# A hybrid decoder step on one core: sums, low parts and evacuations moved in four places

## The chip, the core and the metric

The kernel runs on one core of a Trainium2 chip. TensorE (PE) multiplies matrices into PSUM; VectorE (DVE), ScalarE (ACT) and GpSimd (POOL) work element by element, SyncE (SP) issues the DMAs. Each engine takes its instructions in the order of the program and waits for semaphores of the others. The metric is device time of one launch in microseconds, as the median over runs.

## The reference

The step takes 1024 prompt rows behind 16 meta rows and 8 sample rows, 1048 columns in all, at a width of 1024, in f32:

```
h += 0.5 * SwiGLU_1(rmsnorm(h))            # (silu(x @ wg) * (x @ wu)) @ wd, inner width 2816
u  = rmsnorm(h) @ w_in                     # q, f, i, g of HGRN2; z, x/B/C, dt of Mamba-2
HGRN2 (4 heads of 128): f = lb + (1-lb)*sigmoid(u_f), k = (1-lb)*sigmoid(-u_f), v = u_i, q = silu(u_q)
       S_t = diag(f_t) S_{t-1} + k_t v_t^T, o_t = S_t^T q_t, per-head RMSNorm, * silu(u_g)
Mamba-2 (8 heads of 64, 2 groups, state 128): conv(4) + SiLU, chunked scan
       h_t = exp(dt_t A) h_{t-1} + dt_t x_t B_t^T, y_t = h_t C_t + D x_t, grouped RMSNorm(y * silu(z))
h += concat(hgrn, ssm) @ w_out
h += 0.5 * SwiGLU_2(rmsnorm(h)); final RMSNorm
```

The samples use the same weights, and each has a state of its own: 4 x 128x128 for Mamba-2, read, updated by one step and written back. Outputs are the rows, and the states of prompt and samples.

## The kernel before

Columns are time, partitions are features. Every matrix product is done in three matmuls (`mm3`, L143 to L145): each operand is split into a high part (a cast by ACT) and a low part (what is left, by DVE), and high x high, high x low and low x high are added up in PSUM. Weights are split by `Left.hi` (ACT, L364) and `Left.lo` (DVE, L368), activations by `Blocks.cast` (ACT, L292) and `Blocks.low` (DVE, L298).

**FFNs.** An FFN works through its 2816 inner columns as 22 pairs (gate and up) of 128. A pair is done with seven products instead of eight (a Strassen-like scheme with the numbers 1, 5, 6, 7, 3, 4, 2): sums of weight blocks by `Left.sum_` (DVE, L360), sums of activations by `Blocks.sum_` (L287). Each product is two steps, one for each half c of the columns; a step is twelve matmuls. `Steps` is an order written out by hand: `S.before(i, fn)` issues fn before step i, and the instructions of an engine then run in that order. `Left.plan` sets when loads, sums and splits of a later pair are issued, relative to its first step s0. After a product `post` reads PSUM: product 1 is copied out by ACT (z, L450), 6 and 5 are added by DVE (v, L452; x, L457), 7 gives u1 (L459), 3 gives g1 (L462), each times the norm's factor r where it is complete (`times_r`, L445), 2 gives g0. In the first pair of an FFN, the products come half by half (1, 5, 2, 6, 7, 3 of the first half, then of the second, then 4 twice), since the second half's operands are still being made; there `post_first` holds back the reads of 5 and 2 until 6 and 3 are done. `first2` is the hand-written order of FFN2's first pair, in which `nf2.end` finishes the norm (L211 matmuls, then ACT's logarithm and exponential and DVE's L161 to L163). In `Hidden.jobs` the finished columns are stored (L538) by SP between the weight loads (L354).

**State-space stage.** Behind the input projection of x, B, C and dt a scan runs over nine chunks of 128 columns (`ssm_scan`). Outside the hand-written order a planner places the instructions of an engine by their dependencies. For a chunk SP loads the cumulated decays (L1085, L1092), ACT scales (L1111) and exponentiates them (L1112, L1121), DVE forms the weighted matrix (L1114), PE multiplies (L1118, L1124, L1132), and DVE adds up (L1125, L1126, L1129). PE's projections of HGRN head 0 (q, f, v) are placed between the chunks: `hgrn_project` evacuates each of three column chunks with ACT's Silu (q, L1256) or two Sigmoids (f and k, L1260, L1261). Silu, Sigmoid and Exp need different tables in ACT, and a change of table is an instruction of its own. After each projection three jobs of `K.jobs` are issued: job b updates the state of sample b (loads L1189 and L1190 by SP, L1191, L1195 and L1196 on POOL), reduces it against C (four L1198 on DVE, each writing a product and a sum) and stores it (L1199). The last job adds D x.

**Output.** `ssm_norm` normalises two groups (ACT squares, POOL adds them in L1233, PE sums over partitions in L1237, ACT and DVE finish), the second just ahead of `out_proj`, whose first four units use operands that do not depend on that norm.

Of the kernel before, what the change touches and what calls it, by code (L numbers as in the profile page):

```python
# [12 lines left out]
AF = mybir.ActivationFunctionType  # L13
ALU = mybir.AluOpType
# [328 lines left out]
class Left:  # L343
# [27 lines left out]
        self.hi(p)  # L371
        self.lo(p)

    def plan(self, S, s0, late):
        for ps, ds, fn in (
            ((1, 7, 4, 2), (-10, -10, -9, -9), self.load),
            ((5, 6, 7, 3), (-7, -7, -6, -5), self.sum_),
            (ORDER, [2 * i - 4 + late for i in range(7)], self.split),
        ):
            for p, d in zip(ps, ds):  # L380
                S.before(s0 + d, lambda p=p, fn=fn: fn(p))
# [45 lines left out]
def pair(K, S, wg, wu, f, ops, spread, hid, first=None):  # L427

    nc = K.nc
    fs = slice(f * P, f * P + P)
    s0 = len(S.steps)
    tm = {}
    left = Left(K, [wg[:, 0:4, fs], wu[:, 0:4, fs], wu[:, 4:8, fs], wg[:, 4:8, fs]], 4)

    def temp(n, cs):
        if n not in tm:
            tm[n] = halves(K.t(2 * Q))  # L440
        return tm[n][:, cs]

    def times_r(n, i, cs, src=None):
        t = temp(n, cs)
        nc.vector.tensor_mul(t, t if src is None else src, spread.lanes(i, cs))  # L445
        return t

    def post(p, cs, b):
        if p == 1:
            nc.scalar.copy(temp("z", cs), b)  # L450
        elif p == 6:
            nc.vector.tensor_add(temp("v", cs), b, temp("z", cs))  # L452
        elif p == 2:
            t = times_r("g0", 0, cs, b)
            nc.scalar.activation(t, t, AF.Silu)  # L455
        elif p == 5:
            nc.vector.tensor_add(temp("x", cs), b, temp("v", cs))  # L457
        elif p == 7:
            nc.vector.tensor_add(temp("u1", cs), b, temp("x", cs))  # L459
            times_r("u1", 1, cs)  # L460
        elif p == 3:
            nc.vector.tensor_add(temp("g1", cs), b, temp("v", cs))  # L462
            t = times_r("g1", 1, cs)
            nc.scalar.activation(t, t, AF.Silu)  # L464
        else:
            nc.vector.tensor_add(temp("u0", cs), b, temp("v", cs))
            times_r("u0", 0, cs)
            if "h" not in tm:
                tm["h"] = True
                hid.append(K.slot("s", T))  # L470
            for n in range(2):
                nc.vector.tensor_mul(halves(hid[0][:, n * 2 * Q : n * 2 * Q + 2 * Q])[:, cs], temp(f"g{n}", cs), temp(f"u{n}", cs))

    if not first:
        left.plan(S, s0, int(f == 1))
        Unit(K, left.w, [o.op for o in ops], 4, post).both(S)
        return

    late = {}

    def post_first(p, cs, b):

        if p in (5, 2):
            late[p] = b
        elif p == 7:
            nc.vector.tensor_add(temp("u1", cs), b, temp("x", cs))
        elif p == 3:
            post(2, cs, late[2])
            post(3, cs, b)
            times_r("u1", 1, cs)  # L490
# [658 lines left out]
def ssm_samples(K, a, o):  # L1149
# [32 lines left out]
    sv = a["state_ssm"].rearrange("l b (j f) p n -> l b (f p) j n", f=2)  # L1182
    ov = o["ssm_sample"].rearrange("l b (j f) p n -> l b (f p) j n", f=2)

    def sample(b):
        sb = K.raw().rearrange("p (j n) -> p j n", j=4)
        rw = K.raw()
        rows = rw.rearrange("p (i n) -> p i n", i=4)
        nc.sync.dma_start(sb, sv[0, b])  # L1189
        nc.sync.dma_start(rw, bd[b : b + 1, :].to_broadcast([P, 512]))  # L1190
        nc.gpsimd.tensor_mul(sb, sb, dec[:, :, b : b + 1].broadcast_to([P, 4, P]))  # L1191
        for g in range(2):
            j2 = slice(2 * g, 2 * g + 2)
            up = K.t(2 * P).rearrange("p (j n) -> p j n", j=2)
            nc.gpsimd.tensor_mul(up, rows[:, g, None].broadcast_to([P, 2, P]), dx[:, j2, b : b + 1].broadcast_to([P, 2, P]))  # L1195
            nc.gpsimd.tensor_add(sb[:, j2], sb[:, j2], up)  # L1196
            for j in (2 * g, 2 * g + 1):
                nc.vector.tensor_tensor_reduce(up[:, j % 2], sb[:, j], rows[:, 2 + g], 1.0, 0.0, ALU.mult, ALU.add, ys[:, j, b : b + 1])  # L1198
        nc.sync.dma_start(ov[0, b], sb)  # L1199

    def skip():
        for j in range(4):
            nc.vector.scalar_tensor_tensor(xs[j][:, TP:T], xs[j][:, TP:T], K.dcol[:, j : j + 1], ys[:, j], ALU.mult, ALU.add)

    return [lambda b=b: sample(b) for b in range(NS)] + [skip]


def ssm_gate(K, a, g):
# [16 lines left out]

def ssm_norm(K, g, tag):

    nc = K.nc
    ya, yb = K.y[2 * g], K.y[2 * g + 1]
    v, r = K.slot(tag, w=T), K.slot(tag, w=T)  # L1230
    nc.scalar.activation(v, ya, AF.Square)
    nc.scalar.activation(r, yb, AF.Square)
    nc.gpsimd.tensor_add(v, v, r)  # L1233
    for c0, w in CHUNKS:
        cs = slice(c0, c0 + w)
        ps = K.psm()[:, :w]
# [11 lines left out]
def hgrn_project(K, a, hd, which, jobs=3):  # L1248
# [8 lines left out]

    def ev_f(c0, w, ps):
        f, k = out["f"][:, c0 : c0 + w], out["k"][:, c0 : c0 + w]
        nc.scalar.activation(f, ps, AF.Sigmoid)  # L1260
        nc.scalar.activation(k, ps, AF.Sigmoid, scale=-1.0)  # L1261
        nc.vector.tensor_scalar(f, f, oml, lb, ALU.mult, ALU.add)
        nc.vector.tensor_scalar(k, k, oml, None, ALU.mult)

# [3 lines left out]
    def ev_g(c0, w, ps):  # L1268
        nc.scalar.activation(out["g"][:, c0 : c0 + w], ps, AF.Silu)

    evs = {"q": ev_q, "f": ev_f, "v": ev_v, "g": ev_g}
    ahead = []

    def load(x):
# [181 lines left out]

def out_proj(K, a, h, part, ops, half, after=None):

    wv = a["w_out"][0].rearrange("(b s k p) c -> s p b k c", p=P, s=2, b=2)[part]
    for u in range(4):
        wh, wl = K.weights(wv[:, :, :, u * 256 : (u + 1) * 256])
        for ot in (2 * u, 2 * u + 1):
            os_ = slice((ot % 2) * P, (ot % 2) * P + P)
# [99 lines left out]
def body(ctx, tc, a, o):  # L1565
# [187 lines left out]
    def first2(S, w):  # L1753
# [44 lines left out]
        before(S, 8, (w.split, 4))  # L1798
        return 1, 5, 2, 6, 7, 3, 4

    def after3(S, h, e3, e0, e1):
# [56 lines left out]
```

## Time and profile before

| what | value |
|---|---|
| median of 3 runs | 2137.22 us (2134.08 to 2138.86) |
| profiled execution | 2141.21 us, of which the span from first to last instruction is 2139.4 us |
| mean granted TensorE clock | 0.975 |
| busy: PE, DVE, ACT, POOL | 2021.8, 1491.7, 803.0, 141.3 us |
| steady pairs of FFN1 | 70 to 495 us |
| state-space stage with HGRN head 0's projection | about 870 to 950 us |
| second norm, start of the output projection | about 1295 us |
| FFN2's first pair | 1411 to 1442 us |
| steady pairs of FFN2 | 1442 to 1870 us |

A row of the timeline has the start in us from the span's beginning, the duration, the engine, the line of the kernel, the operation, the tiles and their shape, and in brackets how long the engine had stood idle before and what ended that. A busy share is an average over stages; what a change in a stage is worth is read from the waits of PE in that stage.

### The profile page before, as it was taken

How to read it: one execution, taken by the hardware profiler on the slowest of the kernel's cores; microseconds unless marked ns; L12 is line 12 of the kernel's file. 1: busy time of each engine (PE TensorE's matmuls, PEld its weight loads, DVE VectorE, ACT ScalarE, POOL GpSimd, SP SyncE). 2: the span in 40 equal slices, each digit the busy share in tenths (PEclk: the TensorE clock that was granted, in tenths of full speed). 3: DMA queues.
4: the chain of work that ended last, by engine and by line, in shares of the span. 5: the costliest groups of instructions: out<-in, count | busy, mean ns of one | idle time of the engine just before them, and what ended most of it. 6: DMA issues, size and time to landing. Idle time of an engine off the chain costs nothing.

```text
span 2139.4 us, 38417 instructions
## 1 busy us (share of the span) xinstructions
PE 2021.8 (95%) x15495; PEld 1965.4 (92%) x15495; DVE 1491.7 (70%) x2489; ACT 803.0 (38%) x1494; POOL 141.3 (7%) x175
## 2 busy tenths in 40 slices
PE   5999999999899899799999998979999999989996
PEld 5999999999899889788989997979999999989996
DVE  6777777777787676596454366677777777778863
ACT  7422222223335443562432335652222222324342
POOL 1000000000002110321111010220000000000000
PEclk8999999999999999999999999999999999999999
DMA  6323333246956511452022053313233242587651
GB/s 189 89 81 100 103 93 105 78 131 228 295 165 194 155 47 31 119 154 75 32 71 79 2 176 107 103 60 106 88 107 105 76 120 81 172 265 230 208 166 59
DMA packets 325033, 259.17 MB, mean 121 GB/s; under 512 B 17712, under 2 KB 301104, under 8 KB 324848
## 3 DMA queue, kind: packets, MB, share of 16 engines
q1 hardware_dynamic: 324616, 256.68, 39.5%
q8 instruction: 122, 2.00, 0.4%
q14 instruction: 55, 0.45, 0.1%
q0 software_dynamic: 224, 0.04, 0.0%
q10 hardware_dynamic: 16, 0.00, 0.0%
HBM read 191.26 MB, written 65.47 MB: 120 GB/s over the span
## 4 chain that ended last, share of the span: by engine, by line
PE 78%; DVE 8%; DMA 6%; ACT 3%; issue 2%; SPq 1%; POOL 1%; DVEq 0%; ACTq 0%; POOLq 0%
PE acc L143 24%; PE acc L144 23%; PE acc L145 23%; DMA r<-in_w_ffn_down_dram 2%; DMA r<-in_w_ffn_up_dram 2%; PE mis L1355 2%; DMA u<-hd 1%; DVE s L634 1%; DVE u L287 1%; DVE r L360 1%; PE mis L1394 0%; PE mis L1450 0%; DVE ws L616 0%; DVE u L298 0%; PE mis L1412 0%
## 5 line engine op out<-in xcount | busy, mean ns | idle before, releaser
L143 PE MATMUL acc<-u,ws 128*128 128x262 f32 (+2 forms) x4504 | 1326.9, 296 | 56.5 <-DVE s L634 20.1
L144 PE MATMUL acc<-u,ws 128*128 128x262 f32 (+2 forms) x4504 | 1315.6, 292 | 0.6 <-DVE u L563 0.3
L145 PE MATMUL acc<-u,ws 128*128 128x262 f32 (+2 forms) x4504 | 1313.9, 292 | 1.0 <-DVE ws L368 0.8
L143 PEld LDWEIGHTS acc<-u,ws 128*128 128x128 f32 x4504 | 858.2, 191 | 75.1 <-issue 21.7
L144 PEld LDWEIGHTS acc<-u,ws 128*128 128x128 f32 x4504 | 862.4, 191 | 2.5 <-DVE u L563 0.7
L145 PEld LDWEIGHTS acc<-u,ws 128*128 128x128 f32 x4504 | 858.3, 191 | 1.9 <-DVE ws L368 1.0
L368 DVE TENSOR_TENSOR ws<-r,ws 128x512 fp32r<-128x512 f32 x308 | 212.0, 688 | 103.7 <-ACT ws L364 103.7
L364 ACT CAST ws<-r 128x512 fp32r<-128x512 f32 x308 | 173.3, 615 | 4.7 <-PE acc L145 3.1
L464 ACT ACTIVATE t<-t 128x524 f32<-128x524 f32 (+1 forms) x46 | 28.6, 622 | 313.1 <-DVE t L445 313.1
L360 DVE TENSOR_TENSOR r<-r,r 128x512 f32<-128x512 f32 x176 | 119.1, 697 | 19.0 <-DMA r<-in_w_ffn_up_dram 17.0
L634 DVE SCALAR_TENSOR_TENSOR s<-acc,s 128x524 f32<-128x524 f32 (+1 forms) x120 | 77.6, 663 | 48.8 <-PE acc L145 47.6
L455 ACT ACTIVATE t<-t 128x524 f32<-128x524 f32 (+1 forms) x46 | 28.7, 623 | 216.7 <-DVE t L445 216.7
L204 POOL TENSOR_TENSOR t<-t,t 128x262 f32<-128x262 f32 x56 | 52.9, 960 | 813.2 <-ACT t L203 813.2
L563 DVE TENSOR_TENSOR u<-u,u 128x1048 fp32r<-128x1048 f32 (+1 forms) x84 | 97.1, 1159 | 8.8 <-ACT u L559 8.8
L445 DVE TENSOR_TENSOR t<-t,u 128x524 f32<-128x524 f32 (+1 forms) x138 | 93.6, 681 | 4.7
L138 DVE TENSOR_TENSOR ws<-r,ws 128x512 fp32r<-128x512 f32 x88 | 60.2, 698 | 39.2 <-ACT ws L137 39.0
L611 ACT CAST ws<-r 128x512 fp32r<-128x512 f32 (+1 forms) x84 | 47.8, 581 | 102.9 <-DVE r L606 39.3
L616 DVE TENSOR_TENSOR ws<-r,ws 128x512 fp32r<-128x512 f32 (+1 forms) x84 | 57.2, 691 | 41.6 <-ACT ws L611 41.5
L611 ACT CAST ws<-u 128x512 fp32r<-128x512 f32 (+1 forms) x72 | 42.1, 585 | 113.2 <-DVE u L606 110.9
L559 ACT CAST u<-u 128x1048 fp32r<-128x1048 f32 (+1 forms) x84 | 83.2, 992 | 2.0 <-DMA u<-hd 2.0
L137 ACT CAST ws<-r 128x512 fp32r<-128x512 f32 x88 | 53.8, 617 | 71.7 <-PE acc L145 51.9
L445 DVE TENSOR_TENSOR t<-acc,u 128x524 f32<-128x524 f32 (+1 forms) x46 | 31.3, 680 | 61.6 <-PE acc L145 61.6
(379 smaller groups left out, 1950.1 us busy)
## 6 DMA issues: line engine op xcount, KB each, us to landing
hd<-s SPq DMA_DIRECT2D x170, 262.0 KB
r<-in_w_ffn_down_dram SPq DMA_DIRECT2D x128, 256.0 KB
u<-hd SPq DMA_DIRECT2D x56, 524.0 KB
r<-in_w_ffn_gate_dram SPq DMA_DIRECT2D x88, 256.0 KB
r<-in_w_ffn_up_dram SPq DMA_DIRECT2D x88, 256.0 KB
r<-in_w_in_dram SPq DMA_DIRECT2D x56, 256.0 KB
r<-in_w_ffn_down_dram SPq DMA_DIRECT2D x64, 192.0 KB
u<-hd SPq DMA_DIRECT2D x28, 393.0 KB
```

The costliest lines, as they stand in the source:

```text
L138: self.nc.vector.tensor_sub(lo, src, hi.bitcast(F32))
L143: mm(ps, whi, xhi, start=first, stop=False, skip_group_check=more)
L144: mm(ps, whi, xlo, start=False, stop=False, skip_group_check=more)
L145: mm(ps, wlo, xhi, start=False, stop=last, skip_group_check=more)
L360: self.K.nc.vector.tensor_tensor(self.raw[p], self.raw[x], self.raw[y], op)
L364: self.K.nc.scalar.copy(self.w[p][:, : self.n * P], self.raw[p])
L368: self.K.nc.vector.tensor_sub(t[:, 512 : 512 + w], self.raw[p], t[:, :w].bitcast(F32))
L445: nc.vector.tensor_mul(t, t if src is None else src, spread.lanes(i, cs))
L559: K.nc.scalar.copy(hi, lo.bitcast(F32))
L563: K.nc.vector.tensor_sub(lo, lo.bitcast(F32), hi.bitcast(F32))
L611: nc.scalar.copy(w[p, j, g][:, : n * P], src)
L634: nc.vector.scalar_tensor_tensor(t, b, 0.5, t, ALU.mult, ALU.add)
```

## The change

There are four parts.

- **Pairs of both FFNs** (`plan`, `post`). The loads of a later pair are issued one step earlier, the low part of a weight one step after its cast instead of directly behind it, and in the second pair (f = 1) the sums three steps later. The product u1 times r moves from behind product 7 to behind product 3.
- **FFN2's first pair** (`first2`). The low part of 2, sum 7, the low part of 6, the end of the norm and what follows of the second half move from before steps 2 and 3 to before steps 4, 5 and later, behind the reads of products 6 and 5; the scaling for 3 comes after the weight splits.
- **State-space samples and head 0.** A job updates sample b and then reduces and stores sample b−1; there are nine such jobs and the skip, and four jobs follow each projection of head 0 instead of three. The products of the reductions go to a scratch tile. In head 0 each chunk of q and f leaves PSUM by a plain copy, and Silu and the Sigmoids run once over all columns.
- **Second norm.** `ssm_norm` returns its second half (matmuls, root, scaling), which for the second group is called behind the first unit of the output projection.

```diff
-    def plan(self, S, s0, late):
+    def plan(self, S, s0, late, sums):
-            ((1, 7, 4, 2), (-10, -10, -9, -9), self.load),
-            ((5, 6, 7, 3), (-7, -7, -6, -5), self.sum_),
-            (ORDER, [2 * i - 4 + late for i in range(7)], self.split),
+            ((1, 7, 4, 2), (-11, -11, -10, -10), self.load),
+            ((5, 6, 7, 3), [d + sums for d in (-7, -7, -6, -5)], self.sum_),
+            (ORDER, [2 * i - 4 + late for i in range(7)], self.hi),
+            (ORDER, [2 * i - 3 + late for i in range(7)], self.lo),
...
         elif p == 7:
             nc.vector.tensor_add(temp("u1", cs), b, temp("x", cs))
-            times_r("u1", 1, cs)
         elif p == 3:
             nc.vector.tensor_add(temp("g1", cs), b, temp("v", cs))
             t = times_r("g1", 1, cs)
             nc.scalar.activation(t, t, AF.Silu)
+            times_r("u1", 1, cs)
...
-        left.plan(S, s0, int(f == 1))
+        left.plan(S, s0, int(f == 1), 3 * int(f == 1))
...
-    def sample(b):
+    def update(b):
...
-            for j in (2 * g, 2 * g + 1):
-                nc.vector.tensor_tensor_reduce(up[:, j % 2], sb[:, j], rows[:, 2 + g], 1.0, 0.0, ALU.mult, ALU.add, ys[:, j, b : b + 1])
+        state[b] = sb, rows
+
+    def output(b):
+        sb, rows = state.pop(b)
+        junk = K.t(4 * P).rearrange("p (j n) -> p j n", j=4)
+        for j in range(4):
+            nc.vector.tensor_tensor_reduce(junk[:, j], sb[:, j], rows[:, 2 + j // 2], 1.0, 0.0, ALU.mult, ALU.add, ys[:, j, b : b + 1])
         nc.sync.dma_start(ov[0, b], sb)
+
+    def sample(b):
+        if b < NS:
+            update(b)
+        if b > 0:
+            output(b - 1)
...
-    return [lambda b=b: sample(b) for b in range(NS)] + [skip]
+    return [lambda b=b: sample(b) for b in range(NS + 1)] + [skip]
...
+        nc.scalar.activation(k, ps, AF.Sigmoid, scale=-1.0)
         nc.scalar.activation(f, ps, AF.Sigmoid)
-        nc.scalar.activation(k, ps, AF.Sigmoid, scale=-1.0)
...
+    def ev_raw(x):
+        left = [3]
+
+        def ev(c0, w, ps):
+            nc.scalar.copy(out[x][:, c0 : c0 + w], ps)
+            left[0] -= 1
+            if left[0] == 0:
+                (ev_q if x == "q" else ev_f)(0, T, out[x])
+
+        return ev
+
     evs = {"q": ev_q, "f": ev_f, "v": ev_v, "g": ev_g}
+    if hd == 0:
+        evs.update(q=ev_raw("q"), f=ev_raw("f"))
...
     for u in range(4):
+        if u == 1 and mid:
+            mid()
...
-        u = hgrn_project(K, a, hd, "qfv")
+        u = hgrn_project(K, a, hd, "qfv", 4 if hd == 0 else 3)
...
-            ssm_norm(K, 0, "s")
+            ssm_norm(K, 0, "s")()
...
-    ssm_norm(K, 1, "u")
+    norm1 = ssm_norm(K, 1, "u")
...
-    out_proj(K, a, h, 0, opa, 0)
+    out_proj(K, a, h, 0, opa, 0, mid=norm1)
...
-        e.scaled(h, wn2, (2, 3))
+        e.scaled(h, wn2, (2,))
         w.split(7)
         w.split(3)
+        e.scaled(h, wn2, (3,))
         before(S, 1, (e.cast, 2), (e.sum_, 6))
-        before(S, 2, (e.low, 2), (e.cast, 6), (e.sum_, 7), (nf2.end, 2), (nf2.end, 3, False))
-        before(S, 3, (e.low, 6), (e.cast, 7), (e.sum_, 4))
-        before(S, 4, (e.low, 7), (e.cast, 3))
-        before(S, 5, (e.low, 3), (e.cast, 4))
-        before(S, 6, (e.low, 4), (keep2, 1))
-        before(S, 8, (w.split, 4))
+        before(S, 2, (e.cast, 6))
+        before(S, 4, (e.low, 2), (e.sum_, 7))
+        before(S, 5, (e.low, 6), (nf2.end, 2), (nf2.end, 3, False), (e.cast, 7))
+        before(S, 6, (e.sum_, 4), (e.low, 7), (e.cast, 3))
+        before(S, 7, (e.low, 3), (e.cast, 4))
+        before(S, 8, (e.low, 4), (keep2, 1))
+        before(S, 9, (w.split, 4))
```

In `post_first` the reading of product 7 and the product u1 times r are no longer written out, since `post` now does the same. The first norm calls both halves of `ssm_norm` at once, as before.

More of the change, by code (lines that the diff above doesn't have):

```diff
@@ L484, in post_first @@
             late[p] = b
-        elif p == 7:
-            nc.vector.tensor_add(temp("u1", cs), b, temp("x", cs))
         elif p == 3:
@@ L489, in post_first @@
             post(3, cs, b)
-            times_r("u1", 1, cs)
         else:
@@ L1183, in ssm_samples @@
     ov = o["ssm_sample"].rearrange("l b (j f) p n -> l b (f p) j n", f=2)
-    def sample(b):
+    state = {}
+    def update(b):
         sb = K.raw().rearrange("p (j n) -> p j n", j=4)
@@ L1226, in ssm_norm, with ssm_norm_end @@
 def ssm_norm(K, g, tag):
-    nc = K.nc
     ya, yb = K.y[2 * g], K.y[2 * g + 1]
     v, r = K.slot(tag, w=T), K.slot(tag, w=T)
-    nc.scalar.activation(v, ya, AF.Square)
-    nc.scalar.activation(r, yb, AF.Square)
-    nc.gpsimd.tensor_add(v, v, r)
+    K.nc.scalar.activation(v, ya, AF.Square)
+    K.nc.scalar.activation(r, yb, AF.Square)
+    K.nc.gpsimd.tensor_add(v, v, r)
+    return lambda: ssm_norm_end(K, g, v, r)
+def ssm_norm_end(K, g, v, r):
+    nc = K.nc
     for c0, w in CHUNKS:
@@ L1453, in hgrn_out, with out_proj @@
     nc.vector.tensor_mul(g, g, r)
-def out_proj(K, a, h, part, ops, half, after=None):
+def out_proj(K, a, h, part, ops, half, after=None, mid=None):
     wv = a["w_out"][0].rearrange("(b s k p) c -> s p b k c", p=P, s=2, b=2)[part]
     for u in range(4):
+        if u == 1 and mid:
+            mid()
         wh, wl = K.weights(wv[:, :, :, u * 256 : (u + 1) * 256])
```

## The prediction

> **What bounds the kernel now.** I read the page first, then busy time by stretches, then TensorE's waits in each stretch, and then the timeline around the waits that the change can reach.
>
> ```profile
> span 2139.4 us, 38417 instructions
> PE 2021.8 (95%) x15495; PEld 1965.4 (92%) x15495; DVE 1491.7 (70%) x2489; ACT 803.0 (38%) x1494; POOL 141.3 (7%) x175
> ```
>
> ```profile
> 70.00:495.00 425.00, 423.54 (x3465) 422.68 (x3465) 319.06 (x498) 113.64 (x208) 0.00 (x0) 1.00 0.34 100
> 1442.00:1870.00 428.00, 427.49 (x3498) 426.79 (x3498) 322.19 (x500) 118.53 (x213) 0.00 (x0) 1.00 0.35 105
> 897.00:911.00 14.00, 7.17 (x36) 6.17 (x37) 5.96 (x14) 7.68 (x14) 7.58 (x11) 0.64 0.65 175
> 911.00:930.00 19.00, 17.53 (x120) 15.97 (x120) 18.11 (x34) 12.18 (x24) 10.90 (x13) 0.90 0.63 180
> 930.00:950.00 20.00, 17.89 (x131) 15.67 (x130) 17.69 (x62) 15.30 (x38) 1.73 (x3) 1.00 0.62 185
> ```
>
> The stretch rows give length, then busy time of PE, PEld, DVE, ACT, POOL, then the granted clock. TensorE is the bound: 2021.8 of 2139.4 us. The steady pairs of both FFNs have only 425.00 − 423.54 + 428.00 − 427.49 = 2.0 us of idle TensorE to give. The room is in the state-space stage, where from 897 to 911 us PE works 7.2 of 14 us at a clock of 0.64, and in FFN2's first pair. From 911 to 950 us VectorE is busy 35.8 of 39 us: there it is nearly the bound itself.
>
> ```profile
> PE acc L143 <- DVE t L457: 1.4, 4, 0.5
> PE mis L1118 <- DVE s L1114: 7.6, 2, 6.2
> PE mis L1104 <- DVE s L1125: 5.6, 2, 5.2
> PE mis L1237 <- POOL u L1233: 4.7, 1, 4.7
> PE acc L143 <- ACT t L450: 5.1, 1, 5.1
> ```
>
> These are waits of PE (total, times, longest): the first from 70 to 495 us, the next two from 870 to 960, the fourth from 1280 to 1445, the last from 34 to 70. Each is one that some part of the change aims at.
>
> **State-space stage.** Scan chunk c ends in L1114 and the eight L1118 matmuls; the projection of HGRN head 0 fills PE between chunks.
>
> ```profile
> 892.42 2.44 ACT L1111 ACTIVATE s<-s,s 128x128 f32<-128x128 f32 x8 [3.92 <-DMA s<-cumd]
> 894.88 1.28 ACT L1121 ACT_TABLE_LOAD   x1
> 897.78 1.30 DVE L1114 TENSOR_TENSOR s<-s,s 128x512 f32<-128x512 f32 x2 [1.20 <-ACT s L1112]
> 898.62 1.98 PE L1118 MATMUL mis<-s,s 128*64 128x128 f32 x16 [6.15 <-DVE s L1114]
> 900.53 2.08 PE L1124 MATMUL mis<-u,s 128*128 128x128 f32 x8
> 893.96 1.40 POOL L1196 TENSOR_TENSOR r<-r,t 128x256 f32<-128x256 f32 x2
> 906.33 0.80 DVE L1198 CUSTOM_DVE_ANT_0 t<-r,r 128x128 f32<-128x128 f32 x1 [7.26 <-POOL r L1196]
> 907.06 1.12 DVE L1198 CUSTOM_DVE_ANT_0 t<-r,r 128x128 f32<-128x128 f32 x1
> 909.36 0.68 DVE L1125 TENSOR_TENSOR s<-mis,s 128x512 f32<-128x512 f32 x1
> 910.09 0.69 PE L1104 MATMUL mis<-ident,u 128*128 128x128 f32 x2 [5.21 <-DVE s L1125]
> ```
>
> Chunk 1's wait of 6.15 us ends a chain: SP issues L1085 behind sample 0's store, ACT scales, ACT loads a table (1.28), exponentials, L1114. In the changed order that store and load stand as before, so the scaling still starts at about 892.4. But q's chunk leaves PSUM by a plain copy, no Silu comes between, and the exponential's table is still loaded: L1118 starts 1.3 us earlier, 897.3. The gap keeps 4.8 us, and so probably its slow clock.
>
> The next wait goes wholly. L1125 (it frees the PSUM that L1104 takes) stands behind sample 3's reductions, which wait for POOL, which waited for a state load. In the changed order only sample 2's four reductions stand ahead of it, and their POOL work ended at 893.96 + 1.40 = 895.4. SP also issues sample 3's state load ahead of sample 2's store; a sample's two raw tiles are held one job longer for it, but the weight load that waits for one of them (for v) stands behind a store that waits for POOL until 895.4 anyway. PE is then at L1104 at 904.9 − 1.3 = 903.6 instead of 910.1. What is late next is VectorE's chain for chunk 2:
>
> ```profile
> 939.78 0.69 DVE L1125 TENSOR_TENSOR s<-mis,s 128x512 f32<-128x512 f32 x1 [0.47 <-issue]
> 944.98 1.29 DVE L1114 TENSOR_TENSOR s<-s,s 128x512 f32<-128x512 f32 x2
> 916.10 0.32 PE L145 MATMUL acc<-u,ws 128*128 128x348 f32 x1
> 916.26 0.32 PE L143 MATMUL acc<-u,ws 128*128 128x348 f32 x1
> 917.13 0.66 PE L1118 MATMUL mis<-s,s 128*64 128x128 f32 x8
> ```
>
> From L1125 to the end of the first L1114 it takes 944.98 + 0.65 − 939.78 = 5.9 us undisturbed. It can start when L1124 ends, 900.53 + 2.08 − 1.3 = 901.3, and so is done at 907.2. PE needs 0.7 us for L1104 and L1106 (0.69 for the two L1104 at half clock) and 24 × 0.16 = 3.8 for the projection between, to 908.1. Chunk 2's L1118 comes at 908.0 and not 917.1: 9.1 us, of which 6.5 are the two waits and 2.6 the slow clock that followed the second (0.64 and 0.90 above).
>
> Then VectorE takes some back. Of 32 reductions, before had done 17 by 917.1; the new order has done 12 by then, and two weight splits, as wide as L1125 and so 0.69 each, have moved behind.
>
> ```profile
> L1198 DVE CUSTOM_DVE_ANT_0 t<-r,r 128x128 f32<-128x128 f32 x32 | 14.5, 501 | 9.1 <-POOL r L1196 9.1
> 938.81 0.28 DVE L1198 CUSTOM_DVE_ANT_0 t<-r,r 128x128 f32<-128x128 f32 x1
> ```
>
> A reduction takes 0.28 us alone and up to 1.12 beside POOL, 0.50 on average: five more are 1.4 to 5.6, I take 2.5, and the splits are 1.4. That is 3.9 us in stretches where VectorE has 3.2 of 39 us idle. Sigmoid and its two followers run three chunks at once, which saves a few fixed costs that I leave out. In the chunks 3 and 4 nine and five reductions stand in a row ahead of L1125, so small waits of 1 to 2 us return there. I take 9.1 − 3.9 + 1.3 (a part of the idle) = **6.5 us**, between 2 (contended) and 9.
>
> [...]
>
> **FFN2's first pair.**
>
> ```profile
> 1414.05 1.04 PE L211 MATMUL mis<-t,ones 128*128 128x262 f32 x4
> 1417.75 0.28 PE L145 MATMUL acc<-u,ws 128*128 128x262 f32 x1
> 1417.87 0.28 PE L143 MATMUL mis<-u,ws 128*128 128x262 f32 x1
> 1419.93 0.43 DVE L161 SCALAR_TENSOR_TENSOR t<-t 128x262 f32<-128x262 f32 x1 [1.22 <-ACT t L160]
> 1422.49 1.25 DVE L298 TENSOR_TENSOR u<-u,u 128x1048 fp32r<-128x1048 f32 x1
> 1425.34 0.43 DVE L457 TENSOR_TENSOR t<-acc,t 128x262 f32<-128x262 f32 x1
> 1425.82 0.58 PE L143 MATMUL acc<-u,ws 128*128 128x262 f32 x1 [6.34 <-DVE t L457]
> 1428.84 1.28 ACT L455 ACT_TABLE_LOAD   x1 [0.81 <-DVE t L445]
> 1431.61 0.39 PE L143 MATMUL acc<-u,ws 128*128 128x262 f32 x1 [0.47 <-ACT t L450]
> ```
>
> A step is twelve matmuls of 128x262, start to start 0.12 us: 1.47. The sixth step (product 3) waits 6.34 us for L457, which has five wide operations of VectorE and the norm's root (L161 to L163, twice) ahead of it. In the new order the reads L452 and L457 come as soon as product 6 has ended. That was at 1417.8 (the change of bank from acc to mis), and is some 0.7 earlier now that the norm's matmuls L211 stand behind product 7: the reads run from 1417.2 to 1418.1. PE was through with five steps and the norm at 1425.82 − 6.34 = 1419.5, so step six runs without a wait to 1420.9. But step seven takes the bank that product 2's read frees, and in VectorE's new order there stand low 2, sum 7, one product read, low 6 and the root ahead of it: 1418.1 + 1.25 + 1.25 + 0.43 + 1.25 = 1422.3, the root's six operations 1422.49 − 1419.93 = 2.6, the read 0.4: 1425.2. The wait has moved and is 4.3 us. Step eight needs ACT's copy L450, which before stood behind a table load and two Silus, 1431.61 − 1428.84 = 2.8 us; now a wide cast comes between, about 1 us (an estimate from VectorE's 1.25 for the same width): 1425.2 + 3.8 = 1429.0, and not 1431.61. The clock may still be low then, so of the 2.6 us I take **2.5 us**. Bounds: 0 (the root late by two casts) and 4.5; with no wait at all it would be 1431.61 − 1420.9 − 1.47 = 9.2.
>
> [...]
>
> **Steady pairs.** The fourth load is issued one store earlier, which takes VectorE's sum off a wait for a DMA; the low parts come a step after their casts; one 0.70 multiplication moves behind a Silu.
>
> ```profile
> 270.65 1.42 DVE L360 TENSOR_TENSOR r<-r,r 128x512 f32<-128x512 f32 x2 [1.55 <-DMA r<-in_w_ffn_up_dram]
> 271.98 0.70 DVE L457 TENSOR_TENSOR t<-acc,t 128x524 f32<-128x524 f32 x1
> ```
>
> That sum, 1.55 us late, is what makes L457 late, and L457 makes the 1.4 us of waits in FFN1 and 0.5 in FFN2. Room 2.0, taken **1.5**, or −1 if a low part is now last. Low parts that wait less for their casts give PE nothing more: it is at its rate there. Where the pairs hand over to the down product a further 0.5 us may come, since L462 has 0.70 less ahead of it.
>
> **No gain.** The norm's split: in PE's new order the first norm matmul still stands ahead of the first output product and waits 4.7 us for the same POOL addition. FFN1's second pair: its wait (L450, 5.1) hangs on squares in ACT's queue, not on sums or loads. Both 0, give or take 1.
>
> **The sum.** 6.5 + 2.5 + 1.5 + 0.5 = 11.0 us off the profiled execution's 2141.2 (its span of 2139.4 and 1.8 around it), to 2130.2. The median of the runs shown is 2137.2, 4.0 below that execution, so 2126.2.
>
> **Rivals.**
> - *The stage gives nothing* (0.17): reductions beside POOL at 1.1 us, and nine in a row ahead of L1125, eat the 9 us; for it VectorE's 35.8 of 39, against it the 7.3 us in which it stood idle before them. 2137.2 − 4.5 = 2132.7.
> - *All waits go* (0.10): chunk 1's 4.8 us, the small waits after it and FFN2's 4.3 also vanish with their slow clock: about 12 more, 2114.
> - *Slower* (0.07): in the steady pairs a low part comes after PE wants it. Each pair would wait about one L368, 0.69 us. For it: each low part has one step, 1.47 us, less; against it: VectorE is busy 319 of 425 us. With 41 pairs (425 and 428 us at fourteen steps of 1.47) it costs 28 us and decides from 0.3 us a pair on: 2126.2 + 28 = 2154.
> - *It doesn't do what it says* in the first pair (within the forecast): the wait only moves, which I already count.
>
> **The numbers.** The forecast has 0.66, with a range of its own of 2120 to 2132. The range of 8 in 10 leaves out the slower rival and a part of the best: from 2112, a little under the latter's point, to 2137, where the stage and FFN2's first pair both give nothing. A measurement here tells 0.2%, 4.3 us, from no change, so faster means below 2132.9: the forecast but for a twentieth, the best rival, and half of the first rival make 0.79; the rest of those two and some of the first make 0.13 the same; slower is 0.08.
>
> **What would show it.** Right: no wait on L1125's successor between chunks 1 and 2; L1118 of chunk 2 about 9 us earlier; in FFN2 a wait of 4 to 5 us on a multiplication L446 (g0) one step later than before; steady pairs still at full clock. Wrong: waits of PE on L1114's successor growing in chunks 3 to 5; a wait on L368 in the pairs; FFN2's first pair no shorter.

## The result, and the profile after

The changed kernel takes 2130.88 us (median of 20 runs, 2125.56 to 2135.96) against 2138.24 us (20 runs, 2132.30 to 2145.02) for the kernel before: a ratio of 0.9965, 95% interval 0.9953 to 0.9977, so 7.4 us less. Two later sets of runs of it gave 0.9948 [0.9929, 0.9968] and 0.9963 [0.9945, 0.9980]. The forecast was 2126.2 (2112 to 2137) and 11.0 us less. The profiled execution took 2135.27 us. In what follows lines are those of the changed kernel: L1116 was L1118 before, L1112 was L1114, L1123 was L1125, L1102 was L1104, L1203 was L1198, L446 was L445, L451 was L450, L458 was L457; L462 is L462 in both. e7 and e10 to e12 are shifted against it.

The page of the changed kernel, span and busy time:

```profile
span 2133.6 us, 38427 instructions
PE 2018.2 (95%) x15495; PEld 1962.8 (92%) x15495; DVE 1495.8 (70%) x2485; ACT 801.7 (38%) x1492; POOL 140.4 (7%) x175
```

Its busy time by stretches (length, PE, PEld, DVE, ACT, POOL, granted clock, DMA):

```profile
70.00:495.00 425.00, 423.26 (x3465) 422.65 (x3464) 319.77 (x500) 113.42 (x207) 0.00 (x0) 1.00 0.34 100
897.00:911.00 14.00, 13.15 (x89) 11.37 (x90) 12.99 (x25) 9.64 (x19) 9.34 (x10) 0.84 0.70 203
911.00:930.00 19.00, 15.99 (x109) 14.21 (x108) 18.95 (x51) 13.46 (x28) 12.31 (x15) 1.00 0.65 203
930.00:950.00 20.00, 17.68 (x121) 15.56 (x122) 17.50 (x50) 15.88 (x37) 1.87 (x2) 0.91 0.59 168
1436.00:1864.00 428.00, 425.84 (x3486) 425.20 (x3486) 321.40 (x500) 117.83 (x212) 0.00 (x0) 1.00 0.36 105
```

The span is 5.8 us shorter. The gain shows from 897 to 911 us, where PE now works 13.2 of 14 us and not 7.2. In the rows of the steady pairs PE idles a little more than before, 425.00 − 423.26 + 428.00 − 425.84 = 3.9 us against 2.0; what these pairs gained or lost is counted below over all profiles. VectorE is now the one without room: 18.95 of 19 us from 911 to 930.

PE's waits (total, times, longest): the first two from 865 to 960 us, the next three from 1280 to 1445, the last two from 70 to 495.

```profile
PE mis L1116 <- DVE s L1112: 8.0, 4, 4.6
...
PE mis L1102 <- DVE s L1123: 0.6, 2, 0.4
...
PE mis L1252 <- POOL u L1243: 4.7, 1, 4.7
PE acc L143 <- DVE t L446: 4.1, 1, 4.1
PE acc L143 <- ACT t L451: 2.0, 2, 1.5
...
PE acc L143 <- DVE t L458: 1.3, 2, 1.0
PE acc L145 <- DVE ws L368: 0.4, 1, 0.4
```

Of the two waits of the scan the one for PSUM is gone (5.6 us before, 0.6 now); the wait for L1112 has about the same sum in smaller parts (8.0 us in four, against 7.6 in two). The wait in front of the norm (L1243) is what it was. In FFN2's first pair a wait of 4.1 us stands on the multiplication by the norm's factor, and in the pairs there is a new one, on a low part (L368), in the second pair.

**The scan**, from the timeline of the changed kernel (start, duration, in brackets the idle time before and its end):

```profile
892.20 2.45 ACT L1109 ACTIVATE s<-s,s 128x128 f32<-128x128 f32 x8 [3.66 <-DMA s<-cumd]
896.33 1.29 DVE L1112 TENSOR_TENSOR s<-s,s 128x512 f32<-128x512 f32 x2 [0.83 <-ACT s L1110]
897.17 1.12 PE L1116 MATMUL mis<-s,s 128*64 128x128 f32 x8 [4.63 <-DVE s L1112]
908.03 0.66 PE L1116 MATMUL mis<-s,s 128*64 128x128 f32 x8 [0.69 <-DVE s L1112]
919.61 0.66 PE L1116 MATMUL mis<-s,s 128*64 128x128 f32 x8 [1.97 <-DVE s L1112]
930.30 0.66 PE L1116 MATMUL mis<-s,s 128*64 128x128 f32 x8 [0.72 <-DVE s L1112]
```

Chunk 1 starts at 897.17 with a gap of 4.63 us behind the same late load; chunk 2 at 908.03 where before had 917.13; then 1.97 and 0.72 us come back.

**FFN2's first pair**, same view:

```profile
1408.20 0.39 PE L143 MATMUL acc<-u,ws 128*128 128x262 f32 x1 [0.56 <-ACT t L451]
1412.06 0.43 DVE L458 TENSOR_TENSOR t<-acc,t 128x262 f32<-128x262 f32 x1
1418.77 0.42 DVE L446 TENSOR_TENSOR t<-acc,u 128x262 f32<-128x262 f32 x1
1419.25 0.39 PE L143 MATMUL acc<-u,ws 128*128 128x262 f32 x1 [4.07 <-DVE t L446]
1422.51 0.37 ACT L451 COPY t<-acc 128x262 f32<-128x262 f32 x1
1422.93 0.59 PE L143 MATMUL acc<-u,ws 128*128 128x262 f32 x1 [1.46 <-ACT t L451]
```

The reads of 6 and 5 come at once (done at 1412.5), step six runs without a wait, and steps seven and eight wait 4.07 and 1.46 us. The first row is a wait that the old order hasn't: in step two, for ACT's copy of product 1, which now stands behind the four scalings for 3 (L281, 1.72 us). What this did to the clock is in two rows of the windows, first of before, then of after, for the same part of the pair:

```profile
1419.00:1427.00 8.00, 1.66 (x9) 1.45 (x9) 6.83 (x12) 3.75 (x7) 0.00 (x0) 0.77 0.00 0
1427.00:1436.00 9.00, 8.43 (x57) 7.95 (x56) 7.23 (x12) 4.57 (x7) 0.00 (x0) 0.83 0.01 2
```

```profile
1419.00:1423.00 4.00, 2.29 (x13) 1.98 (x13) 3.97 (x7) 2.31 (x5) 0.00 (x0) 0.66 0.01 4
1423.00:1427.00 4.00, 4.00 (x18) 4.00 (x19) 2.74 (x3) 1.98 (x3) 0.00 (x0) 0.50 0.00 0
```

Before, a part of the slow clock fell into the wait of 6.34 us, where it costs nothing (0.77 while PE worked 1.66 of 8 us). After, it falls on steps at work: 18 matmuls in the 4 us from 1423 to 1427, against 35 in the 4 us behind.

### The profile page after: what moved, and what is told of

Same layout as the page of the kernel before. It is cut to its first block, busy times and chain, and to the rows that moved or that the text cites. A ratio compares the mean times of both kernels' runs of the same rounds, so it can differ in the third digit from the quotient of the medians.

```text
span 2133.6 us, 38427 instructions
## 1 busy us (share of the span) xinstructions
PE 2018.2 (95%) x15495; PEld 1962.8 (92%) x15495; DVE 1495.8 (70%) x2485; ACT 801.7 (38%) x1492; POOL 140.4 (7%) x175
## 4 chain that ended last, share of the span: by engine, by line
PE 76%; DVE 10%; DMA 4%; ACT 3%; issue 3%; SPq 1%; POOL 0%; DVEq 0%; ACTq 0%; POOLq 0%
PE acc L143 23%; PE acc L144 23%; PE acc L145 23%; PE mis L1383 1%; DMA r<-in_w_ffn_up_dram 1%; DMA u<-hd 1%; DVE s L632 1%; DMA r<-in_w_ffn_down_dram 1%; DVE t L446 1%; DVE u L561 1%; DVE ws L614 1%; DVE s L473 1%; DVE s L1397 1%; DVE ws L368 1%; DVE s L1385 0%
## 5 line engine op out<-in xcount | busy, mean ns | idle before, releaser
L143 PEld LDWEIGHTS acc<-u,ws 128*128 128x128 f32 x4504 | 859.1, 191 | 73.0 <-issue 21.9
L368 DVE TENSOR_TENSOR ws<-r,ws 128x512 fp32r<-128x512 f32 x308 | 212.5, 690 | 75.2 <-ACT ws L364 75.0
L360 DVE TENSOR_TENSOR r<-r,r 128x512 f32<-128x512 f32 x176 | 122.2, 697 | 13.1 <-DMA r<-in_w_ffn_up_dram 11.3
L632 DVE SCALAR_TENSOR_TENSOR s<-acc,s 128x524 f32<-128x524 f32 (+1 forms) x120 | 77.6, 663 | 48.9 <-PE acc L145 47.6
L446 DVE TENSOR_TENSOR t<-t,u 128x524 f32<-128x524 f32 (+1 forms) x138 | 89.9, 679 | 3.3
L446 DVE TENSOR_TENSOR t<-acc,u 128x524 f32<-128x524 f32 (+1 forms) x46 | 31.3, 680 | 60.9 <-PE acc L145 60.9
```

The source lines that it names most:

```text
L143: mm(ps, whi, xhi, start=first, stop=False, skip_group_check=more)
L360: self.K.nc.vector.tensor_tensor(self.raw[p], self.raw[x], self.raw[y], op)
L368: self.K.nc.vector.tensor_sub(t[:, 512 : 512 + w], self.raw[p], t[:, :w].bitcast(F32))
L632: nc.vector.scalar_tensor_tensor(t, b, 0.5, t, ALU.mult, ALU.add)
```

## The experiments

Each run's own profile differs from the next by some us even where the code is the same, so I compare stages and not spans. Every one of these traces holds the same 15495 matmuls of PE, and the time between the starts of two of them, counted from the beginning, is the length of a stage whatever was gained or lost ahead of it. In us, by that count:

```
matmuls        stage                           before  after     e1     e2     e3     e4     e5     e6     e7     e8     e9    e10    e11    e12
200 - 400      FFN1, end of pair 1, pair 2       28.4   30.4   28.6   28.5   30.5   27.8   29.3   27.3   30.4   29.2   30.4   27.8   30.4   30.4
400 - 3800     FFN1, steady pairs, hand-over    419.3  417.9  420.5  418.2  417.2  419.0  416.2  419.3  416.9  416.6  415.9  418.5  417.7  417.8
3800 - 5800    FFN1 down, projections           277.4  278.3  276.9  275.8  273.6  275.2  276.1  275.5  274.0  277.1  274.8  275.3  278.7  278.5
5800 - 7000    state-space stage                196.9  191.0  189.6  191.5  195.3  195.0  189.9  190.0  189.6  199.1  190.5  190.0  190.6  188.3
7000 - 9800    heads, output projection         415.8  415.1  413.6  413.9  414.9  415.0  414.0  417.7  414.9  411.5  413.6  413.9  410.7  410.8
9800 - 9900    FFN2, up to step two of pair 1    14.9   15.6   14.8   14.8   14.8   15.6   15.6   15.6   15.6   15.6   15.6   15.6   15.6   15.6
9900 - 10000   FFN2, most of pair 1              21.9   20.9   22.6   21.7   22.5   21.5   21.4   21.2   21.3   21.2   21.3   21.4   21.5   21.0
10000 - 10200  FFN2, end of pair 1, pair 2       24.4   25.5   24.4   24.4   25.5   24.4   25.5   24.4   25.5   25.5   25.5   24.4   25.5   25.5
10200 - 13600  FFN2, steady pairs, hand-over    418.3  418.0  418.2  419.3  416.5  418.5  416.1  418.6  417.4  416.7  416.4  416.4  418.4  417.0
```

The timed runs, in three sets, each on one chip with runs of the kernel before beside them:

| run | what it holds | median us | ratio to before, 95% |
|---|---|---|---|
| before (35 runs) | | 2136.67 | |
| e1_ssm | samples and raw copies alone | 2131.13 | 0.9974 [0.9960, 0.9988] |
| e2_sums | samples alone | 2133.49 | 0.9985 [0.9971, 0.9999] |
| e3_plan | pairs' plan alone | 2132.97 | 0.9977 [0.9964, 0.9990] |
| e4_first2 | FFN2's first pair alone | 2135.48 | 0.9994 [0.9981, 1.0007] |
| before (33 runs) | | 2137.92 | |
| e5_whole | the whole change | 2125.71 | 0.9948 [0.9929, 0.9968] |
| e6_noplan | without the pairs' plan | 2131.21 | 0.9967 [0.9955, 0.9980] |
| e7_root | first pair's norm split up further | 2128.73 | 0.9956 [0.9938, 0.9974] |
| e8_pst | sample states stored by POOL | 2137.12 | 0.9998 [0.9981, 1.0015] |
| before (25 runs) | | 2135.96 | |
| e9_whole2 | the whole change | 2129.72 | 0.9963 [0.9945, 0.9980] |
| e10_lo_early | low parts behind their casts again | 2125.50 | 0.9953 [0.9940, 0.9965] |
| e11_load_late | loads one step later again | 2132.74 | 0.9983 [0.9974, 0.9992] |
| e12_u1_early | u1's multiplication behind product 7 again | 2131.61 | 0.9977 [0.9964, 0.9990] |

### The state-space part alone, and its sums alone

The kernel before, with the third part of the change; and with the jobs on samples only:

```diff
+    def output(b):
+        sb, rows = state.pop(b)
...
+            output(b - 1)
```

> The kernel before with the state-space part alone (sums of a sample behind the next sample's update, plain copies of q and f in head 0). Theory: this part carries the whole gain: PE reaches the stage after it 5.9 us earlier and a further 0.7 is won in the heads behind it, so 6 to 7 us less than before (ratio 0.997), and chunk 2's first L1116 matmul stands near 908 us. Rival (the gain is spread over the parts): 2 to 4 us less, and no more than the whole change has.

> The kernel before with only the samples' sums moved behind the next sample's update (nine jobs, four behind each projection of head 0), and Silu and Sigmoids chunk by chunk as before. Theory: the 5.2 us wait on DVE's sum of scan chunk 1 goes with its slow clock, but chunk 1's wait stays at 6.1 us, since ACT still loads a table there: 4 to 5 us less than before. Rival (the table loads held the stage, not the sums): 0 to 1 us less.

Measured: 2131.13 and 2133.49 us against 2136.67. e1's 5.5 us less (interval 2.6 to 8.5) lies between its theory and its rival and fits either; e2's 3.2 (0.2 to 6.2) is nearer to its theory than to its rival. By the count of matmuls the stage takes 196.9, 195.3 and 195.0 us in the three profiles with the old samples (before, e3, e4), 195.7 in the mean, 191.5 in e2, and 190.0 in the mean of the nine with samples and copies (all others but e8). The sums give 4.2 us, the copies about 1.5, of which the spread of one profile is a good part. In e2 PE's waits from 865 to 960 us read:

```profile
PE mis L1118 <- DVE s L1114: 6.0, 4, 5.1
PE mis L1104 <- DVE s L1125: 2.8, 2, 2.3
```

and in its timeline:

```profile
895.22 2.05 PE L1118 MATMUL mis<-s,s 128*64 128x128 f32 x16 [5.06 <-DVE s L1114]
910.47 0.44 PE L1104 MATMUL mis<-ident,u 128*128 128x128 f32 x2 [0.45 <-DVE s L1125]
931.68 0.44 PE L1104 MATMUL mis<-ident,u 128*128 128x128 f32 x2 [2.32 <-DVE s L1125]
```

With the samples alone PE no longer waits at L1104 between chunks 1 and 2 (both rows of L1104 come later); chunk 1's wait is 5.06 us, where 6.1 were expected; a wait of 2.32 us on the same line comes back later, at 931.68 us. So it was the order of VectorE's reductions that held PSUM, as the prediction had it.

### The pairs' plan alone, and the whole without it

> The kernel before with only the orders of the pairs of both FFNs changed (loads a step earlier, low parts a step behind casts, sums of the second pair three steps later, u1 times r behind Silu). Theory: these cost instead of gaining: a low part is late once in each FFN (0.4 and 0.7 us) and the sum that waits for the fourth load is no earlier, so 0.5 to 1.5 us more than before. My prediction: 2 us less.

> The whole change without the new orders of the pairs (plan, and where u1 times r stands). Theory (the pairs' part is worth nothing, since PE is at its rate there, and the 5 us that it showed alone are the spread of the runs): within 1.5 us of the whole change. Rival (the pairs' part is worth 3 to 5 us, though the steady stretch doesn't show it): 3 to 5 us more than the whole change.

Measured: the plan alone gains 3.7 us (2132.97 against 2136.67, interval 2.1 to 7.7); left out of the whole it costs 5.5 (2131.21 against 2125.71). By the timed runs both theories fall, and both values are more than the prediction's 1.5 + 0.5. The profiles show where, and not all of it. The hand-over to the down product loses its wait on L462 in both FFNs (0.6 each). The steady pairs of the two FFNs, hand-over included, take 832.3 to 835.9 us together in the six profiles with the plan as in after (after, e3, e5, e7, e8, e9; 833.6 in the mean) and 837.5 to 838.7 in the five without (before, e1, e2, e4, e6; 837.8): 4.2 us less. But the stretches in which the second pair starts are longer, 30.1 against 28.1 and 25.5 against 24.4 us in the mean of the same profiles: 3.0 us more. By the profiles the plan is thus worth 1.2 us, by the timed runs 4 to 5 us. The difference may lie in stretches that the plan does not touch, which vary without any change to them: by 5 us from matmul 3800 to 5800 and by 7 from 7000 to 9800, where e6 has the longest (417.7 us, 3.7 above e5). That is not shown.

### FFN2's first pair alone

> The kernel before with only the order of FFN2's first pair changed. Theory: the wait moves from step six to step seven and is 4.1 us, and the slow clock that had fallen on waiting steps now falls on working ones: the pair is 0.3 us shorter, within 0.5 us of before. My prediction: 2.5 us less.

Measured: 2135.48 against 2136.67, not to be told from no change, as the theory had it. By the count the pair takes 21.5 against 21.9 us from matmul 9900 on. But the new wait of 0.56 us lies ahead of that: from 9800 to 9900 every profile with the new order takes 15.6 us and every one with the old 14.8 or 14.9. From 9800 to 10000 the nine with the new order (all but e7) take 36.9 us in the mean and the four with the old (before, e1, e2, e3) 37.0: the order is worth about 0.2 us.

### The whole again, and the norm of FFN2's first pair split up further

> The whole change once more, beside the next three on the same chip. Theory (the state-space part carries the gain) and its rival (the pairs' orders carry as much): both the same, 7 us less than before.

Measured: 2125.71 us, 12.2 less than before where 7 were expected; the interval, 6.8 to 15.2, just holds that.

In e7 the norm's matmuls, logarithm and exponential come early on PE and ACT, VectorE's six operations right behind the reads of 6 and 5, and the second half's low parts and sums behind the reads of 2 and 3:

```diff
+        before(S, 1, (e.cast, 2), (e.sum_, 6), (nf2.end_act, (2, 3)))
...
+        before(S, 4, (nf2.end_dve,))
+        before(S, 6, (e.low, 2), (e.low, 6), (e.sum_, 7), (e.cast, 7), (e.sum_, 4), (e.low, 7), (e.cast, 3))
```

> The whole change, and in FFN2's first pair the norm's matmuls, logarithm and exponential go on PE and ACT behind step 1 ahead of the cast of 6, its six operations on DVE directly behind the reads of 6 and 5, and low 2, sum 7 and low 6 behind the reads of 2 and 3. Theory (step seven waits for the wide operations and the root ahead of product 2's read): step seven's wait falls from 4.1 us to between 1 and 2, and the pair is 2 to 4 us shorter than in the whole change; low parts that come late may put up to 1.5 us back in steps ten to twelve. Rival (the slow clock behind any wait, not the wait, sets the pair's length): within 1 us of the whole change.

Measured: 2128.73 against 2125.71, each within the other's spread. By the count the pair takes 36.9 us from matmul 9800 to 10000, as in the whole change: the theory's 2 to 4 us did not come. PE's waits in the pair, in e7:

```profile
PE acc L143 <- ACT t L474: 5.4, 1, 5.4
...
PE acc L143 <- DVE t L469: 1.6, 1, 1.6
```

The wait on the multiplication (L469 in that kernel) falls from 4.1 to 1.6 us, and the next one rises from 0.7 (in e5) to 5.4: ACT's copy of product 1 (L474) stands behind casts that wait for VectorE's sums. VectorE works almost without a pause there (13.9 of the 14.3 us from 1404.5 to 1418.8 in e7), so this order of its work moved the wait and didn't shorten the pair. That no order would is not shown.

### The states stored by POOL

This takes the store, which waits for POOL, out of SP's queue, so that chunk 1's load of decays is not behind it:

```diff
-        nc.sync.dma_start(ov[0, b], sb)
+        nc.gpsimd.dma_start(ov[0, b], sb)
```

> The whole change, with the stores of the samples' states issued by POOL, behind its own addition, and not by SP. Theory (chunk 1's wait of 4.6 us stands because SP holds the load of the decays, L1083, behind the first store, which waits for POOL): that load is issued 4 to 5 us earlier, the wait falls below 1.5 us and its slow clock goes with it, so 3 to 6 us less than the whole change. Rival (ACT's and DVE's work for the chunk is late by itself, or POOL loses as much by issuing): within 1.5 us of the whole change.

Measured: 2137.12 us, 11.4 above the whole, where the theory had 3 to 6 less; the stage takes 199.1 us by the count. From its timeline:

```profile
885.82 1.48 POOL L1195 TENSOR_TENSOR t<-r,s 128x256 f32<-128x256 f32 x2
886.77 3.16 DVE L1203 CUSTOM_DVE_ANT_0 t<-r,r 128x128 f32<-128x128 f32 x1
...
895.58 1.12 PE L1116 MATMUL mis<-s,s 128*64 128x128 f32 x8 [5.17 <-DVE s L1112]
...
910.43 1.12 PE L1116 MATMUL mis<-s,s 128*64 128x128 f32 x8 [4.85 <-DVE s L1112]
```

and the group of reductions from 870 to 985 us, in this kernel and in the changed one:

```profile
L1203 DVE CUSTOM_DVE_ANT_0 t<-r,r 128x128 f32<-128x128 f32 x32 | 20.5, 689 | 0.0
```

```profile
L1203 DVE CUSTOM_DVE_ANT_0 t<-r,r 128x128 f32<-128x128 f32 x32 | 14.3, 493 | 0.0
```

With SP freed POOL waits for state loads 4.6 us in this stage (11.6 in e5), one reduction takes 3.16 us where one alone takes 0.28, and all 32 take 20.5 us and not 14.3. Chunk 1 now waits for VectorE, which is at reductions until 894.75, instead of for the load, and chunk 2 waits 4.85 us too. The stores in SP's queue had held back the state loads behind them, and so POOL. How much of the lengthening is POOL's arithmetic and how much its issuing of DMAs was not told apart.

### The three edits of the plan, each undone

```diff
-            (ORDER, [2 * i - 4 + late for i in range(7)], self.hi),
-            (ORDER, [2 * i - 3 + late for i in range(7)], self.lo),
+            (ORDER, [2 * i - 4 + late for i in range(7)], self.split),
```

is e10; e11 has the loads at −10, −10, −9, −9 again, e12 the multiplication `times_r("u1", 1, cs)` behind product 7.

> The changed kernel once more, as the anchor for the three runs beside it, each of which takes one of the three edits out of the pairs' plan. Both theories: 2126 to 2131 us; in the profile a wait on L368 at the first steady pair of each FFN (0.4 to 1.2 us), none on L462.

> The changed kernel, but each low part of a weight is made directly behind its cast again, as before. Theory (the pairs' plan gains by single waits, and the low parts' own share is about nothing): the wait on L368 at the first steady pair of each FFN goes (0.4 to 1.2 us each), and about 1 us of waits on L457's and L458's reads returns: within 1.5 us of the whole change. Rival (the low parts carry the 4 to 5 us that the plan was worth in the timed runs): 4 to 5 us above the whole change.

> The changed kernel, but the pairs' four loads are issued one step later, as before. Theory: the fourth load landed no earlier in the changed kernel, and the sum L360 waited for it all the same (1.97 us against 1.55), so nothing moves: within 1.5 us of the whole change, and that sum waits 1.5 to 2.5 us for the DMA. Rival (the earlier loads carry the plan's gain, as the prediction had it): 3 to 5 us above the whole change, with waits on L457 as in the kernel before (1.4 us in FFN1's pairs).

> The changed kernel, but in the steady pairs and the first ones the 0.70 us multiplication for u1 stands behind product 7's read again, ahead of product 3's, as before. Theory: the wait of 0.6 us on L462 at each hand-over to the down product returns, 1.2 us in all, and nothing else: 1 to 1.5 us above the whole change. Rival (this multiplication delays a bank in every pair, and its move carries the plan's gain): 4 to 5 us above the whole change, with waits on product 3's read inside the pairs.

*Low parts.* e10 took 2125.50 us against 2129.72: the late low parts carry none of the gain, and the rival falls. The theory's 1.5 us is missed on the other side: by the means of the runs e10 is 4.0 us faster, with an uncertainty of 3. The waits on L368 are gone and 1.8 us on L457's read return. By the count e10 gets back the whole loss at the second pairs (27.8 and 24.4 us), and gives up 2.6 us against e9 in FFN1's steady pairs, 1.7 against the mean of the six profiles named above. A part of e9's 2.6 us at FFN1's second pair is the clock. It shows in two rows of each trace, PE's second wait in the first pair and the clock behind it, for e9 and then for e10:

```profile
63.39 1.20 PE L906 MATMUL mis<-t,ones 128*128 128x262 f32 x4 [3.15 <-ACT t L900]
```

```profile
65.00:69.00 4.00, 4.00 (x24) 4.00 (x24) 3.63 (x6) 2.42 (x5) 0.00 (x0) 0.64 0.00 0
```

```profile
63.00 1.20 PE L905 MATMUL mis<-t,ones 128*128 128x262 f32 x4 [2.36 <-ACT t L899]
```

```profile
65.00:69.00 4.00, 4.00 (x35) 4.00 (x34) 3.96 (x8) 1.82 (x3) 0.00 (x0) 1.00 0.00 0
```

The low parts do not settle the clock: with the code of e9 in this pair the gap is 1.9 us in e8 and 2.5 in e5. The clock fell behind it in e8, in before, e1 and e2 (1.8 to 2.0 us), and in the six profiles with 3.1 to 3.2 us, but not in e4, e5, e6 and e10 (2.2 to 2.6 us); what decided it was not shown. Where it fell, the stretch takes 29.2 to 30.5 us with late low parts and 28.4 to 28.6 with early ones; where it did not, 29.3 (e5) and 27.3 to 27.8. So at the same clock the late low parts cost about 1.7 us there in the mean, of which the wait on L368 is 0.4 us (1.2 in e5); the rest was not traced.

*Loads.* e11 took 2132.74 us, 3.0 above e9; the interval 0.9974 to 0.9992 overlaps e9's a little. By the count FFN1's and FFN2's steady pairs take 836.2 us together: 3.8 above e9, but 2.5 above the mean of the six profiles with the same pairs, of which the highest (after) has 835.9. VectorE's idle time ahead of the sums L360 in FFN1's pairs that a load ended (us, times) is, in before, e9 and e11:

```profile
  DMA r<-in_w_ffn_up_dram: 9.7, 11
```

```profile
  DMA r<-in_w_ffn_up_dram: 4.3, 9
```

```profile
  DMA r<-in_w_ffn_up_dram: 7.9, 10
```

So my theory for this run, that the fourth load lands no earlier, falls: it came from one pair (270 us), and over all pairs the earlier issue takes 3.6 to 5.4 us of such waits off VectorE. In the other traces in which the loads come early these waits are 4.1 to 6.1 us (7.8 in e10), and 8.5 to 11.6 where they come late. The rival, which was the prediction's mechanism, stands; its size, 2.5 to 3 us, is less certain.

*u1.* e12 took 2131.61 us, 1.9 above e9, and the two waits of 0.6 us at the hand-over are back, as the theory had it; the intervals of the timed runs overlap widely. The count agrees: the hundred matmuls from 3700 to 3800, over FFN1's hand-over, take 13.5 us in every profile with the multiplication behind product 3 and 14.2 in every other, e12 among them.

## Why the prediction was right, and where it was not

- **The state-space term: right.** 6.5 us were predicted; 5.7 is what the stage gave by the count (195.7 to 190.0 us in the means). The steps came as worked out: chunk 1 at 897.17 (predicted 897.3) with a gap of 4.63 (4.8), chunk 2 at 908.03 (908.0), small waits of 0.7 to 2 us after that. Of these the larger is not where the prediction put it: the 1.97 us stand ahead of chunk 3, and behind the nine reductions in a row (from 920.53 us) only 0.72 us come. The term's subtraction was partly beside the point: 2.5 us for five more reductions in a contended stretch. All 32 reductions take 14.3 us after and 14.5 before. One takes 0.28 us alone, and the mean of the 32 is 0.49 after and 0.50 before: they were lengthened as much in the old order, and more in e8 (20.5 us, 0.69 in the mean), where POOL waits less for loads and issues the stores.
- **FFN2's first pair: the step that failed is the last, "the clock may still be low then, so of the 2.6 us I take 2.5".** The waits came out as worked out (step seven 4.07 us, predicted 4.3; step eight at 1422.93, predicted 1429.0 less the 6.5 us gained ahead, 1422.5). Step eight thus came 2.2 us earlier within the pair. But the shorter wait let PE back to work while the clock was low (0.66 from 1419 to 1423 us, 0.50 from 1423 to 1427, the latter at full work), and at the pair's end 0.3 us were left in after, 0.2 in the mean of all profiles. The prediction also put nothing on the scaling for 3, which costs a wait of 0.56 us in step two. So the term is about nothing where 2.5 us were taken.
- **Steady pairs: the mechanism was right, a term was missing.** The earlier load is worth about 2.5 to 3 us (e11) where 1.5 were taken, because the row quoted was one of eleven such waits. What was not counted is the start: low parts and sums that come later in the second pair cost 1.9 us in FFN1 and 1.1 in FFN2 by the count, of which waits on L368 are 0.4 and 0.7. With it the plan is worth some 1.2 us by the count, hand-over included. The rival "low part late" named the right wait, but it comes once in an FFN and not in each pair.
- **Hand-over: right in kind, too small.** 0.5 predicted; 0.6 in each FFN, 1.2 in all.
- **Norm's split and FFN1's second pair at nothing:** right for the norm by its wait (4.7 us before and after), though no run has this part alone; FFN1's second pair lost 1.9 us, the cost just named, which is outside the give or take of 1.
- **The clock behind a gap.** That the 4.8 us of chunk 1 would keep their slow clock was right: the gap of 4.63 us has 0.50 from 894.6 to 901.4 us. Behind 4.07 us (after, 0.66 from 1419 to 1423) and 3.15 us (e9, 0.64 from 65 to 69) the clock was low too, behind 2.36 (e10, 1.00 from 65 to 69) and 1.97 us (chunk 3, 1.00 from 911 to 930) it was not. But it was low behind 2.50 us in before (last section), and behind 1.8 us in before's first pair of FFN1 (0.50 from 64.8 to 68.2). Here the length of the gap alone does not decide.

The three sets gave 7.4, 12.2 and 6.2 us less, 8.6 in the mean, against the 11.0 of the forecast; the stages sum to 5.7 + 0.2 + 1.2 = 7.1 us by the count. What is short lies mostly in FFN2's first pair and the second pairs. The forecast lies 4.7 us under the measured median, 1.0 of which is that before's median was taken as 2137.2 and came out as 2138.24. The range holds the result because the largest term was right and because it was wide enough for one of 2.5 us to be nothing. Two of the prediction's signs of being wrong did come, a wait on L368 (once in each FFN) and a first pair of FFN2 that is hardly shorter. Why the plan is worth 4 to 5 us in timed runs and 1.2 in the profiles stays open. e10, the change with its low parts directly behind their casts, had the lowest median of all (2125.50 us, five runs) and is the version to go on with; that it beats the whole change is likely, not certain.

## What to carry to other kernels

When a wait on PSUM ends a gap, look for work in the reader's queue that waits for a third engine, and move that work behind the read: here four reductions set a sample later freed 4 us with no work saved. A wait that is shortened but not removed can be worth next to nothing: in FFN2's first pair 6.34 us became 4.07 a step later, the slow clock behind it (0.50 from 1423 to 1427 us) then fell on work instead of on the gap, and about 0.2 us were left. Cost such a wait with the granted clock of the steps that follow. Size an edit to a repeated loop by the sum over all its rounds, not by the one wait whose row is at hand.

## What the runs showed of the hardware

The same gap was not followed by the same clock in every profile. Behind a wait of 2.50 us in the down product (L634 before, L632 in the changed kernel) the clock fell in before and not in e9. Before:

```profile
741.10 0.59 PE L143 MATMUL acc<-u,ws 128*128 128x262 f32 x1 [2.50 <-DVE s L634]
```

```profile
742.00:744.00 2.00, 2.00 (x11) 2.00 (x11) 1.89 (x4) 0.30 (x1) 0.46 (x1) 0.50 0.98 344
```

and e9:

```profile
737.64 0.39 PE L143 MATMUL acc<-u,ws 128*128 128x262 f32 x1 [2.49 <-DVE s L632]
```

```profile
736.00:739.00 3.00, 1.36 (x11) 1.36 (x12) 2.92 (x7) 1.15 (x3) 0.81 (x1) 1.00 0.81 218
```

In before the first thirteen matmuls behind the gap take 2.99 us up to the start of the fourteenth, 0.22 us from start to start in most; in e9 the same thirteen take 1.71 us, 0.12 from start to start. By this spacing the clock fell in seven of the fourteen profiles (before, after, e1, e2, e8, e11, e12) and stayed full in the other seven. The stage from matmul 3800 to 5800 took 275.8 to 278.7 us in the first seven and 273.6 to 276.1 in the others. After and e9 are the same kernel, with 278.3 us in this stage where the clock fell and 274.8 where it did not. What decided it was not shown. So a difference of a microsecond or two between two profiles in this stage need not come from an edit. The clock explains little of the 10 us by which runs of one kernel differ: the profiles of after and e9 have the same mean granted clock, 0.978, and their spans, 2133.6 and 2124.3 us, are 9.3 us apart.
